# Columns of the weights' sums cast by ScalarE, spaced splits, and raw loads kept behind the conv tiles' loads

## The chip, the cores and the metric

The kernel runs on one core of a Trainium2 chip. The metric is the device time of one execution in microseconds. A core has five engines that run side by side, each in the order of its own instructions: TensorE (PE, matmuls, with its weight loads as PEld), VectorE (DVE), ScalarE (ACT), GpSimd (POOL) and SyncE (SP), which here issues the DMAs. They wait for each other through semaphores.

## The reference

One encoder block on x of 1024 tokens by 1024 channels in float32. Cut to what matters here:

```python
u = rms_norm(x, norm1_g)
q, k, v, cb, cc, ch, ga, gb = split(u @ w_in)
y_a = neighbourhood_attention(q, k, v, rpb) @ w_attn_branch
y_b = short_gated_conv(cb, cc, ch, conv_w) @ w_conv_branch
merged = sigmoid(ga) * y_a + sigmoid(gb) * y_b
x = x + merged @ w_o
h = rms_norm(x, norm2_g) @ w_mlp_in
x = x + square(relu(h)) @ w_mlp_out
```

The change touches the work on the gates `ga`, `gb` and on the two branch products.

## The kernel before, in words

float32 matmuls are done as float16 ones: each operand is split in a high half and a low half (`hi = fp16(w * s)`, `lo = fp16(w * s - hi)`), and products hi·hi, hi·lo and lo·hi are added in PSUM. A unit of 128 channels by 512 tokens is 12 matmuls of 128x512 in the gates and the attention branch, and 6 in the conv branch. The scale `s` of a weight chunk is a power of two made from the sum of the squares of the chunk. Parts of the products go by sums of blocks (a fast form with seven products, `seven`), so the splits are made of the raw weights, of their sums `gsum` (POOL, L1325) and, for the conv branch, of raw blocks added by POOL (L1414).

The preparation of a chunk goes like this. SP loads 128x1024 float32 weights into a `raw` buffer (L269, `load_now`; `due` decides when one is put in SP's program). ACT scales them by rows (L1201) where a norm belongs in, and takes squares with a sum for each partition (L1210, and L1396 for the conv branch). DVE adds the two or four sums of a partition (L1178, L394), and casts the result to one bf16 column of the tile `ones` (L1179, L396). PE multiplies a 128x128 block of ones by this column (L236 in `all_sum`), which adds over the partitions. DVE makes the scale from that (L239, then L495 to L502 or L160 to L163 and L327, and L1402 for the conv branch). Then come the splits: ACT casts the high half (L1343), DVE subtracts for the low half (L1339); `parts` gives them out in turn, a high half ahead of the low half before it. For the attention branch weights (`w_wa`) the two are L367 and L354, and their row sums of squares are one DVE reduction of 128x1024 (L386).

The stage is from about 310 to 560 us. Its PE program is written by loops: `gate_units(n)` makes the units of gate chunk n with the weights `w_s`; `a_unit` those of the attention branch with `w_wa`; `ab(j)` the units of both branches, in an order such as `"bb0b1bbb2b3"`, where b is a conv unit (weights `w_wb`, tile `bT`, which SP loads from the DRAM tile `bf`, L1519) and a digit an attention unit. The preparation steps are generators (`prep_s`, `prep_b`, `Chunk.prep`), put in a background queue `bg`; `tick` and `apart` place their instructions between the units by the number of PE columns that have been issued (6144 columns are a unit of 12 matmuls of 512). So the position of each instruction on its engine is fixed when the program is built, and an instruction that waits holds up all behind it on its engine. `cA[j]` are the attention branch chunks, `prep_b(j)` the conv branch's, and `prep_s(n)` the gates'. At the end of a chunk's use the sigmoid runs on ACT (L1498, tile `sg`, after sums on DVE at L1487 to L1496). Early in the stage, ACT and DVE also make the conv tiles: L943, L946, L961 to L988 on `bT`, `zb`, `mH`, `mL`.

Of the kernel before, what the change touches and what calls it, by code (L numbers as in the profile page):

```python
# [12 lines left out]
BF16 = mybir.dt.bfloat16  # L13
I32 = mybir.dt.int32
AF = mybir.ActivationFunctionType
# [86 lines left out]
def encoder_block(ctx: ExitStack, tc: tile.TileContext, x, weights, cols, gqk, rel, masks, out):  # L102
# [108 lines left out]
    def apart(mark, n=3, of=units):  # L211
        while of[0] < mark + n and not forced[0]:
            yield WAIT

    def built(*chs):
# [9 lines left out]
            tick()  # L225
            step()
        forced[0] = False
    ones, turn = base.tile([128, 132], BF16, name="ones"), [0]
    V.memset(ones, 1.0)

    def ones_col():
        turn[0] = (turn[0] + 1) % 4
        return ones[:, 128 + turn[0]:129 + turn[0]]

    def all_sum(a, out, bk, floor, lag=1):
        T.matmul(bk[:, 0:1], ones[:, 0:128], a, start=True, stop=True)  # L236
        yield
        yield from apart(units[0], lag)
        V.tensor_scalar(sc[:, out], bk[:, 0:1], floor, None, op0=OP.max)  # L239
        yield  # L240
# [27 lines left out]
        m = ch.widths[p][0] * ch.widths[p][1]  # L268
        SP.dma_start(t, bass.AP(tensor=weights.tensor, offset=weights.offset + ch.offs[p], ap=[[m, 128], [1, m]]))  # L269

    pend, deferring = [], [False]

    def due():
        while pend and (forced[0] or pend[0][0] <= work[0]):
            load_now(pend.pop(0)[1])

    def load_upto(n):
# [14 lines left out]
    class Chunk:  # L292
# [11 lines left out]
        def prep(self):  # L304
# [2 lines left out]
            rm, a, b, s = (cols_of("prep", i) for i in (nk, 1, 1, 1))  # L307
            self.inv = keep()
            tot = sum(k * w for k, w in self.widths)
            if self.kind in "QKCG":  # L310
                self.parts = wsp.tile([128, 2, tot], F16, name="w16_ws", tag="ws")
                for p, (k, w) in enumerate(self.widths):
                    while len(self.raw) <= p:
                        yield WAIT
                    A.activation(self.parts[:, 1, :k * w].bitcast(BF16), self.raw[p][:, :k * w], AF.Square,
                                 accum_out=sc[:, at(rm, p)])
                    yield
                V.tensor_reduce(sc[:, a], sc[:, at(rm, 0, n)], axis=AX, op=OP.add)
                c = ones_col()
                V.tensor_tensor(c, sc[:, a], sc[:, gm2], op=OP.mult)  # L320
                yield from apart(units[0], {"Q": 2, "C": 2, "K": 1}.get(self.kind, 3))
                yield from all_sum(c, b, bank(self.bank) if self.bank else anybank(), 1e-36)
                yield from pow2_half(b, 14, s, self.inv, more=self.more)
            else:
                yield from self.largest(rm, a, b)
                yield from pow2(b, 14, s, self.inv, False, more=self.more)
# [1002 lines left out]
        ch.sum = sum_of(sm)  # L1329
        yield  # L1330

    def parts(todo, s, then):

        scale = (lambda n: s[n]) if isinstance(s, list) else lambda n: s
        prev = None
        for n, it in enumerate(todo + [None]):
            if prev:
                o, w = prev
                V.scalar_tensor_tensor(o(1), w, sc[:, scale(n - 1)], o(0), op0=OP.mult, op1=OP.subtract)  # L1339
                then(n - 1)  # L1340
            if it:
                o, w = it
                A.activation(o(0), w, AF.Copy, scale=sc[:, scale(n)])  # L1343
            prev = it
            yield

    def forms_split(ch, t, s, P, turned=False):

        def then(n):
            if n == 1 and ch is not c1[0]:  # L1350
                done[0] += 2
                load_upto(done[0] + 5)
        r = ch.r
        todo = [(0, 1, r[0][:, 0:1]), (1, 3, r[1]), (3, 5, t[:, 0:2]), (5, 7, t[:, 2:4])]
        if turned:
            todo[2:] = todo[:1:-1]
        yield from parts([((lambda i, a=a, b=b: P[:, a:b, i]), w) for a, b, w in todo], s, then)

    gates = [0]

    def prep_s(n):

        ch = cS[n]
        if n == 1:
            while ch.s is None:
                yield WAIT
            s = ch.s
        else:
            yield from rows_scaled(ch, g1)
            sm = yield from squares(ch, M[0][:, 7].bitcast(BF16))  # L1370
            yield from apart(work[0], 2 * 6144, work)
            am = sum_of(sm)
            yield
            s, ch.inv = yield from scale_of(am, 9, 2)
        while done[0] < ch.first or n > 1 and not cS[n - 1].split or gates[0] < n - 1:
            yield WAIT
        t = w3p.tile([128, 4, 512], F32, name="gsum", bufs=1)
        yield from forms_sum(ch, t, None)
        if n > 1:
            yield from apart(work[0], 6144, work)  # L1380
        ch.P = wsp.tile([128, 7, 2, 512], F16, name="w16_s", tag="ws")
        yield from forms_split(ch, t, s, ch.P, n == 1)
        ch.split = True

    PB, pairs = {}, [0]
# [1 line left out]
    def prep_b(j):  # L1387

        ch = cB[j]
        while not ch.raw or not rowed[0] or not aged(ch, 0):  # L1390
            yield WAIT
        raw = ch.raw[0]
        w = raw.rearrange("p (a e n c) -> p e n a c", a=2, e=2, n=2)
        sm, rm = cols_of("prep", 2), cols_of("prep", 2)
        for a in range(2):
            A.activation(M[0][:, 7, :512].bitcast(BF16), raw[:, 512 * a:512 * a + 512], AF.Square,  # L1396
                         scale=sc[:, at(rowsB, a)], accum_out=sc[:, at(sm, a)])
        yield from apart(work[0], 2 * 6144, work)
        am = sum_of(sm)
        yield  # L1400
        s, ch.inv = yield from scale_of(am, 0, 3 if j else 2)
        V.tensor_scalar(sc[:, rm], sc[:, at(rowsB, 0, 2)], sc[:, s], None, op0=OP.mult)  # L1402
        yield
        while pairs[0] < j or done[0] < ch.first:
            yield WAIT
        P = PB[j] = wab.tile([128, 7, 2, 256], F16, name="w16_wb", tag="wb", bufs=1)

        def place(f, g, a):
            return lambda i: P[:, f:g, i, 128 * a:128 * a + 128]
        yield from parts([x for a in range(2) for x in ((place(0, 1, a), w[:, 0, 0:1, a]), (place(1, 3, a), w[:, 1, :, a]))],  # L1410
                         [at(rm, a) for a in (0, 0, 1, 1)], lambda n: None)
        for o, x_, y_ in (((0, 0), (0, 0), (0, 1)), ((0, 1), (0, 1), (1, 1)), ((1, 1), (0, 0), (1, 1)),
                          ((1, 0), (1, 1), (1, 0))):
            G.tensor_tensor(w[:, o[0], o[1]], w[:, x_[0], x_[1]], w[:, y_[0], y_[1]], op=OP.add)  # L1414
        yield from apart(work[0], 2 * 6144 if j else 6144, work)
        yield from parts([x for a in range(2) for x in ((place(3, 5, a), w[:, 0, :, a]), (place(5, 7, a), w[:, 1, :, a]))],
                         [at(rm, a) for a in (0, 0, 1, 1)], lambda n: None)
        done[0] += 1
        load_upto(done[0] + 5)
        ch.split = True  # L1420
# [150 lines left out]
    def ab(j):  # L1571
        n, P, ps = 2 * j, PB[j], {}
        z = [zb[:, i] for i in range(4)]

        def post2():
            V.tensor_tensor(z[0], ps[2], z[1], op=OP.add)
            times(n, 0)

        def post7():
            V.tensor_tensor(z[2], ps[7], z[1], op=OP.add)  # L1580
            V.tensor_tensor(z[1], ps[5], z[1], op=OP.subtract)
            V.tensor_tensor(z[3], ps[5], z[2], op=OP.subtract)
            V.tensor_tensor(z[2], ps[4], z[2], op=OP.add)
            times(n, 1)
            times(n + 1, 1)

        def post3():
            V.tensor_tensor(z[1], ps[3], z[1], op=OP.add)
            times(n + 1, 0)
        posts = {1: lambda: A.activation(z[1], ps[1], AF.Copy),  # L1590
                 6: lambda: V.tensor_tensor(z[1], ps[6], z[1], op=OP.add), 2: post2, 7: post7, 3: post3}

        def b_unit(o):
            i = ORDB[o]
            w = {5: 6, 6: 5}.get(SEVEN[i][1], SEVEN[i][1])
            act = SLOT[:, (7 * j + o) % 4]
            ps[i] = anybank()
            unit(group(ps[i], [(P[:, w, sw, 128 * a:128 * a + 128], act[:, a, sa]) for a in range(2)
                               for sw, sa in PASSES]), posts.get(i), 2, 4)
            land(7 * j + o + 4)  # L1600
        order = "bb0b1bbb2b3"
        if j == 0:
            order = "bb2b3bbbb"
        o = 0
        for c in order:
            if c == "b":
                b_unit(o)
                o += 1
            else:
                a_unit(n + int(c) // 2, int(c) % 2)  # L1610
        pairs[0] = j + 1

    tick(8)
    bg.append(prep_s(1))
    tick(2)
    fg.append(first_forms())
    bg.append(prep_b(0))
    for j in range(1, 4):
        bg.append(prep_s(2 * j))
        push(cA[j])  # L1620
# [690 lines left out]
```

## Time and profile before

| | us |
|---|---|
| three runs, median | 1216.38 |
| three runs, lowest and highest | 1215.01, 1217.11 |
| the profiled execution | 1214.99 |
| its span in the trace | 1213.2 |
| busy: PE | 1191.6 |
| busy: PEld | 574.6 |
| busy: DVE | 962.0 |
| busy: ACT | 777.8 |
| busy: POOL | 482.3 |

Busy times are sums over the span of one engine; PE is busy in 98% of it. Register, branch, semaphore and DMA-issuing instructions are not counted. The mean granted clock of PE was 0.994. Times in rows of the trace are from the span's start. In a row such as `ps_d<-ones`, the name at the left is the tile that is written, the ones at the right are read.

### The profile page before, as it was taken

The page shows a single profiled execution, that of the slowest core. Times are in us where ns is not written, and L with a number is a line of the kernel's source. Part 1 is how long each engine was busy: PE and PEld are TensorE (multiplying, and loading weights), DVE is VectorE, ACT ScalarE, POOL GpSimd, SP SyncE. Part 2 cuts the span into 40 slices and gives each one's busy share as a digit, 9 for nine tenths or more (in the row PEclk, how much of TensorE's full clock was granted, in tenths as well). Part 3 has the DMA queues.
Part 4 walks back from the last instruction along what each step waited for, and adds up shares of the span by engine and source line. Part 5 has one row for each costly group of instructions (what it writes and reads, how often), then busy time and mean ns, then how long its engine had stood idle before and what let it go on. Part 6 is the DMA issues. An engine that isn't in the chain of part 4 may idle for free.

```text
span 1213.2 us, 17139 instructions
## 1 busy us (share of the span) xinstructions
PE 1191.6 (98%) x6248; PEld 574.6 (47%) x6248; DVE 962.0 (79%) x1793; ACT 777.8 (64%) x1241; POOL 482.3 (40%) x314
## 2 busy tenths in 40 slices
PE   8999999999988998999999999999999999999998
PEld 7444444445433443444458444444444444444444
DVE  7987877898778887877878656456448989999998
ACT  7775668778656755436668787687775754646440
POOL 5610020221424360411003765665657562464472
PEclk9999999999998999999999999999999999999999
DMA  7755646787774424315096555355375924435212
GB/s 264 196 156 117 112 108 123 146 159 134 152 277 154 156 72 148 129 61 234 17 184 157 182 191 175 125 178 178 123 280 181 354 106 170 174 109 224 101 38 105
DMA packets 168373, 189.62 MB, mean 156 GB/s; under 512 B 123616, under 2 KB 124128, under 8 KB 164192
## 3 DMA queue, kind: packets, MB, share of 16 engines
q1 hardware_dynamic: 168288, 188.52, 52.0%
q8 instruction: 49, 0.80, 0.3%
q14 instruction: 36, 0.29, 0.1%
HBM read 117.19 MB, written 41.42 MB: 131 GB/s over the span
## 4 chain that ended last, share of the span: by engine, by line
PE 87%; DVE 8%; ACT 2%; issue 1%; POOL 1%; DMA 1%; DVEq 0%; ACTq 0%; POOLq 0%
PE ps_d L245 26%; PE ps_s L245 23%; PE ps_o L245 19%; PE ps_d L1166 9%; PE ps_d L695 2%; PE ps_d L744 2%; PE ps_s L744 2%; DVE w_s L1339 2%; PE ps_s L695 2%; PE ps_o L1147 1%; PE ps_s L1071 1%; POOL gsum L1325 1%; DVE w_wb L1339 1%; ACT raw L1201 1%; DMA bT<-bf 1%
## 5 line engine op out<-in xcount | busy, mean ns | idle before, releaser
L245 PEld LDWEIGHTS <-ops 128*128 128x128 f16 x1356 | 132.4, 98 | 157.3
L245 PEld LDWEIGHTS <-w 128*128 128x128 f16 x1368 | 132.8, 98 | 139.5
L1166 PE MATMUL ps_d<-uT,w_ws 128*128 128x512 f16 x576 | 127.9, 379 | 0.0
L245 PE MATMUL ps_s<-ops 128*128 128x512 f16 (+1 forms) x528 | 119.7, 377 | 0.0
L245 PE MATMUL ps_d<-ops 128*128 128x512 f16 x480 | 110.1, 379 | 0.0
L2132 ACT ACTIVATE ops<-hf,sc 128x2048 f16<-128x2048 f32 x26 | 52.0, 1998 | 84.8 <-PE ps_s L245 37.7
L1325 POOL TENSOR_TENSOR tsum<-raw 128x512 f32<-128x512 f32 x28 | 48.2, 1737 | 139.6 <-DVE v L1760 74.1
L1710 POOL TENSOR_TENSOR as<-as 128x512 f32<-128x512 f32 x60 | 82.9, 1381 | 41.6 <-ACT as L1992 38.1
L245 PEld LDWEIGHTS <-w_s 128*128 128x128 f16 x588 | 58.0, 100 | 80.8 <-issue 16.0
L1166 PEld LDWEIGHTS <-w_ws 128*128 128x128 f16 x576 | 54.5, 98 | 65.2 <-issue 1.0
L245 PE MATMUL ps_d<-u2T,w 128*128 128x512 f16 (+1 forms) x360 | 78.8, 368 | 0.0
L245 PE MATMUL ps_o<-ops 128*128 128x512 f16 (+1 forms) x348 | 78.6, 375 | 0.0
L2134 DVE SCALAR_TENSOR_TENSOR ops<-hf,sc,ops 128x2048 f16<-128x2048 f32 x26 | 74.4, 2861 | 3.3 <-ACT ops L2132 3.2
L245 PE MATMUL ps_o<-u2T,w 128*128 128x512 f16 (+1 forms) x348 | 76.0, 368 | 0.0
L245 PE MATMUL ps_s<-u2x,w 128*128 128x512 f16 (+1 forms) x336 | 74.5, 371 | 0.0
L1201 ACT ACTIVATE raw<-raw,sc 128x256 f32<-128x256 f32 x164 | 67.8, 493 | 1.9 <-DMA raw<-in_weights 1.9
L1343 ACT ACTIVATE w<-raw,sc 128x512 f16<-128x512 f32 (+1 forms) x28 | 24.6, 927 | 51.0 <-DVE sc L501 51.0
L2025 DVE TENSOR_TENSOR as<-ps_s,as 128x512 f32<-128x512 f32 x13 | 9.0, 692 | 57.9 <-ACT as L2044 57.9
L2148 POOL TENSOR_TENSOR raw<-raw 128x1024 f32<-128x1024 f32 x8 | 30.8, 3868 | 36.6 <-DVE ops L2142 36.6
L245 PEld LDWEIGHTS <-mH 128*128 128x128 f16 x304 | 29.6, 98 | 30.5
L2106 POOL TENSOR_TENSOR t<-raw,w2x 128x1024 f32<-128x1024 f32 x6 | 18.7, 3114 | 62.0 <-DMA w2x<-in_weights 62.0
L2138 ACT ACTIVATE ops<-raw,sc 128x1024 f16<-128x1024 f32 x24 | 26.3, 1138 | 26.6 <-DVE sc L152 19.2
(441 smaller groups left out, 2744.3 us busy)
## 6 DMA issues: line engine op xcount, KB each, us to landing
raw<-in_weights SPq DMA_DIRECT2D x89, 512.0 KB, 5.5
hs<-as SPq DMA_DIRECT2D x16, 1792.0 KB, 8.0
hf<-hs SPq DMA_DIRECT2D x26, 1024.0 KB, 6.2
bT<-bf SPq DMA_DIRECT2D x28, 512.0 KB, 4.5
w2x<-in_weights SPq DMA_DIRECT2D x16, 512.0 KB, 7.8
raw<-in_weights SPq DMA_DIRECT2D x16, 384.0 KB, 3.6
xt<-in_x SPq DMA_DIRECT2D x8, 512.0 KB, 10.9
gs<-s SPq DMA_DIRECT2D x4, 1024.0 KB, 4.4
```

The costliest lines, as they stand in the source:

```text
L245: T.matmul(ps, l, r, start=a, stop=b)
L695: T.matmul(ps, UT[:, sa, k, b * 128:(b + 1) * 128], w, start=(kind, k) == ("hh", 0), stop=(kind, k) == ("hl", 7))
L744: T.matmul(vbank["q", b], UT[:, sa, k, b * 128:(b + 1) * 128], cQ.parts[:, sw, 512 * k:512 * k + 512], start=(k, n) == (0, 0), stop=(k, n) ...
L1166: T.matmul(ps, l, r, start=a, stop=b)
L1201: A.activation(v, v, AF.Copy, scale=sc[:, at(g, 4 * i + k)])
L1325: G.tensor_tensor(t[:, o], a, b, op=OP.add)
L1339: V.scalar_tensor_tensor(o(1), w, sc[:, scale(n - 1)], o(0), op0=OP.mult, op1=OP.subtract)
L1710: sub.tensor_tensor(z[o], z[a], z[b], op=op)
L2132: A.activation(P[:, 1, 0], hf, AF.Copy, scale=sc[:, Rs])
L2134: V.scalar_tensor_tensor(P[:, 1, 1], hf, sc[:, Rs], P[:, 1, 0], op0=OP.mult, op1=OP.subtract)
L2138: A.activation(P[:, 0, 0, 1024 * i2:1024 * i2 + 1024], w[i2], AF.Copy, scale=sc[:, fw])
L2148: G.tensor_tensor(w11[i2], w11[i2], w12[i2], op=OP.add)
```

## The change

1. The column of a weights' sum is no longer added and cast on DVE. `summed(sums)` casts the two or four partial sums on ACT into two or four columns of `ones`, and `all_sum` multiplies each column on PE and adds them in PSUM. `prep_s` (from chunk 2), `prep_b` and `cA[1]` to `cA[3]` use it. For these `cA` the sums of squares are four ACT squares of 128x256 in place of the DVE reduction.
2. The waits in columns between the squares and the sum go away; in their place the sum is put at once behind the cast, and the `ones` matmul where the distance from it says.
3. Splits of `prep_s` (from chunk 2) and `prep_b` are spaced (`gap=1`): the high halves of a pair or a group on ACT, then 6144 columns of PE work, then the low halves on DVE.
4. In `ab`, raw loads are kept out of SP's program while the first conv tiles' loads are put in (`behind`).
5. `prep_b(0)` is put in the queue ahead of `prep_s(1)`, with two more ticks.

In counts: ACT gets 25 more instructions of the kind ACTIVATE (13 casts, 12 squares), DVE loses 16 reductions and 13 casts, PE gets 19 more `ones` matmuls with their weight loads; POOL and SP have as many instructions as before.

```diff
-    ones, turn = base.tile([128, 132], BF16, name="ones"), [0]
+    ones, turn = base.tile([128, 148], BF16, name="ones"), [0, 0]
...
+    def summed(sums):
+        n = sums.stop - sums.start
+        if turn[1] + n > 16:
+            turn[1] = 0
+        turn[1] += n
+        a = 132 + turn[1] - n
+        nc.scalar.activation(ones[:, a:a + n], sc[:, sums], AF.Copy)
+        return [ones[:, a + i:a + i + 1] for i in range(n)]
+
     def all_sum(a, out, bk, floor, lag=1):
-        T.matmul(bk[:, 0:1], ones[:, 0:128], a, start=True, stop=True)
+        a = a if isinstance(a, list) else [a]
+        for i, c in enumerate(a):
+            T.matmul(bk[:, 0:1], ones[:, 0:128], c, start=i == 0, stop=i == len(a) - 1)
...
     def due():
-        while pend and (forced[0] or pend[0][0] <= work[0]):
+        while pend and not (behind[0] and not forced[0]) and (forced[0] or pend[0][0] <= work[0]):
             load_now(pend.pop(0)[1])
...
-            if self.kind in "QKCG":
+            if self.kind == "A" and self is not cA[0]:
+                while not self.raw or not aged(self, 0):
+                    yield WAIT
+                sm = cols_of("prep", 4)
+                for i in range(4):
+                    A.activation(M[0][:, 7, :256].bitcast(BF16), self.raw[0][:, 256 * i:256 * i + 256], AF.Square,
+                                 scale=sc[:, at(self.rows, i)], accum_out=sc[:, at(sm, i)])
+                c = summed(sm)
+                yield
+                yield from apart(work[0], 3 * 6144, work)
+                yield from all_sum(c, b, anybank(), 1e-36)
+                yield from pow2_half(b, 14, s, self.inv)
+            elif self.kind in "QKCG":
...
-    def parts(todo, s, then):
+    def parts(todo, s, then, gap=0):
 
+        if gap:
+            get = (lambda n: s[n]) if isinstance(s, list) else lambda n: s
+            for n, (o, w) in enumerate(todo):
+                A.activation(o(0), w, AF.Copy, scale=sc[:, get(n)])
+                yield
+            yield from apart(work[0], gap * 6144, work)
+            for n, (o, w) in enumerate(todo):
+                V.scalar_tensor_tensor(o(1), w, sc[:, get(n)], o(0), op0=OP.mult, op1=OP.subtract)
+                then(n)
+                yield
+            return
...
-            sm = yield from squares(ch, M[0][:, 7].bitcast(BF16))
-            yield from apart(work[0], 2 * 6144, work)
-            am = sum_of(sm)
-            yield
-            s, ch.inv = yield from scale_of(am, 9, 2)
+            sm = cols_of("prep", 2)
+            for i in range(2):
+                A.activation(M[0][:, 7].bitcast(BF16), ch.raw[i], AF.Square, accum_out=sc[:, at(sm, i)])
+                yield
+            c = summed(sm)
+            s, ch.inv = yield from scale_of((c, work[0]), 9, 3)
...
-        yield from apart(work[0], 2 * 6144, work)
-        am = sum_of(sm)
-        yield
-        s, ch.inv = yield from scale_of(am, 0, 3 if j else 2)
+        c = summed(sm)
+        yield
+        s, ch.inv = yield from scale_of((c, work[0]), 0, 3 if j else 2)
...
             land(7 * j + o + 4)
+            behind[0] = o < 2
+        behind[0] = True
         order = "bb0b1bbb2b3"
...
     tick(8)
-    bg.append(prep_s(1))
+    bg.append(prep_b(0))
+    tick(2)
+    bg.insert(0, prep_s(1))
     tick(2)
     fg.append(first_forms())
-    bg.append(prep_b(0))
```

Two places show how instructions move. The first is ACT about 326 to 342 us, from the row scales of a raw gate chunk on (`raw<-raw`). The casts `w_wb` are the high halves of the first conv branch weights, `L1210` and, after, `L1411` the squares of gate chunk 2. Line numbers after are 11 to 40 higher. Before:

```order
L1201 ACTIVATE raw<-raw,sc 128x2x128 x4
L943 ACTIVATE mH<-bT 128x512 x2
L1481 ACTIVATE sg<-raw 128x512
L1478 ACTIVATE sg<-ps_d,sc 128x512
L943 ACTIVATE mL<-bT 128x512 x4
L1201 ACTIVATE raw<-raw,sc 128x2x128 x4
L1210 ACTIVATE mH,sc<-raw 128x1024 x2
L1201 ACTIVATE raw<-raw,sc 128x2x128 x4
L1509 ACTIVATE sg<-ps_s 128x512
L1343 ACTIVATE w_wb<-raw,sc 128x128
```

And after, from the squares of `cA[1]` on, which stand right behind the first of those row scales:

```order
L326 ACTIVATE mH,sc<-raw,sc 128x256 x4
L241 ACTIVATE ones<-sc 128x4
L966 ACTIVATE mH<-bT 128x512 x2
L1518 ACTIVATE sg<-raw 128x512
L1515 ACTIVATE sg<-ps_s,sc 128x512
L966 ACTIVATE mL<-bT 128x512 x4
L1360 ACTIVATE w_wb<-raw,sc 128x128
L1360 ACTIVATE w_wb<-raw,sc 128x2x128
L1360 ACTIVATE w_wb<-raw,sc 128x128
L1360 ACTIVATE w_wb<-raw,sc 128x2x128
L1224 ACTIVATE raw<-raw,sc 128x2x128 x4
L1411 ACTIVATE mH,sc<-raw 128x1024 x2
```

The four `w_wb` casts were behind the squares of gate chunk 2 and are now ahead of them and of the row scales before these; the cast `L241 ACTIVATE ones<-sc 128x2` for the sum follows right behind the last row. `cA[1]`'s squares and its cast of four columns are new in the row.

The second place is SP from about 342 to 373 us, in `ab(0)`: the loads of conv tiles (`bT`) and of raw weights. Before:

```order
L1519 DMA bT<-bf 128x2048 x4
L269 DMA raw<-in_weights 128x1024
L1519 DMA bT<-bf 128x2048 x2
L269 DMA raw<-in_weights 128x1024 x2
L1519 DMA bT<-bf 128x2048
L269 DMA raw<-in_weights 128x1024
L1519 DMA bT<-bf 128x2048 x4
```

After:

```order
L1556 DMA bT<-bf 128x2048 x4
L280 DMA raw<-in_weights 128x1024
L1556 DMA bT<-bf 128x2048 x3
L280 DMA raw<-in_weights 128x1024 x3
L1556 DMA bT<-bf 128x2048 x4
```

The seventh `bT` load stood behind two raw loads and has moved ahead of them; the three raw loads now go out together.

More of the change, by code (lines that the diff above doesn't have):

```diff
@@ L269, in load_into @@
         SP.dma_start(t, bass.AP(tensor=weights.tensor, offset=weights.offset + ch.offs[p], ap=[[m, 128], [1, m]]))
-    pend, deferring = [], [False]
+    pend, deferring, behind = [], [False], [False]
     def due():
-        while pend and (forced[0] or pend[0][0] <= work[0]):
+        while pend and not (behind[0] and not forced[0]) and (forced[0] or pend[0][0] <= work[0]):
             load_now(pend.pop(0)[1])
@@ L1345, in parts, with forms_split @@
             yield
-    def forms_split(ch, t, s, P, turned=False):
+    def forms_split(ch, t, s, P, turned=False, spaced=False):
         def then(n):
@@ L1356, in forms_split @@
             todo[2:] = todo[:1:-1]
+        if spaced:
+            at_p = [((lambda i, a=a, b=b: P[:, a:b, i]), w) for a, b, w in todo]
+            yield from parts(at_p[:2], s, lambda n: then(n), 1)
+            yield from parts(at_p[2:], s, lambda n: None, 1)
+            return
         yield from parts([((lambda i, a=a, b=b: P[:, a:b, i]), w) for a, b, w in todo], s, then)
@@ L1378, in prep_s @@
         yield from forms_sum(ch, t, None)
-        if n > 1:
-            yield from apart(work[0], 6144, work)
         ch.P = wsp.tile([128, 7, 2, 512], F16, name="w16_s", tag="ws")
-        yield from forms_split(ch, t, s, ch.P, n == 1)
+        yield from forms_split(ch, t, s, ch.P, n == 1, n > 1)
         ch.split = True
@@ L1410, in prep_b @@
         yield from parts([x for a in range(2) for x in ((place(0, 1, a), w[:, 0, 0:1, a]), (place(1, 3, a), w[:, 1, :, a]))],
-                         [at(rm, a) for a in (0, 0, 1, 1)], lambda n: None)
+                         [at(rm, a) for a in (0, 0, 1, 1)], lambda n: None, 1)
         for o, x_, y_ in (((0, 0), (0, 0), (0, 1)), ((0, 1), (0, 1), (1, 1)), ((1, 1), (0, 0), (1, 1)),
@@ L1416, in prep_b @@
         yield from parts([x for a in range(2) for x in ((place(3, 5, a), w[:, 0, :, a]), (place(5, 7, a), w[:, 1, :, a]))],
-                         [at(rm, a) for a in (0, 0, 1, 1)], lambda n: None)
+                         [at(rm, a) for a in (0, 0, 1, 1)], lambda n: None, 1)
         done[0] += 1
```

## The prediction

> **What bounds the kernel now.** I began with the table of busy time by stretch, then the waits of TensorE (PE), and then followed each wait to the engine that ended it. The first view shows, for each stretch, the span and PE's busy time, then PEld, VectorE (DVE), ScalarE (ACT) and GpSimd (POOL), the granted clock, the DMA share and GB/s.
>
> ```profile
> 309.00:345.00 36.00, 30.80 (x143) 13.81 (x142) 30.88 (x49) 28.22 (x53) 14.70 (x12) 0.98 0.79 225
> 345.00:400.00 55.00, 49.96 (x218) 21.87 (x217) 46.27 (x101) 35.00 (x62) 24.89 (x22) 0.92 0.45 157
> 400.00:460.00 60.00, 56.42 (x266) 25.50 (x264) 48.47 (x100) 33.63 (x59) 24.88 (x18) 1.00 0.38 123
> ```
>
> PE lacks 5.20, 5.04 and 3.58 us there, 13.82 us in all. So PE sets the time, and in this stage it is stopped by others. All that the change can win is here. The waits of PE from 300 to 670 us name the four places:
>
> ```profile
> PE ps_d L245 <- DMA bT<-bf: 5.0, 1, 5.0
> PE ps_o L236 <- DVE ones L1179: 3.6, 1, 3.6
> PE ps_d L236 <- DVE ones L396: 3.6, 1, 3.6
> PE ps_d L236 <- DVE ones L1179: 1.6, 1, 1.6
> ```
>
> Three are the one-column `ones` matmul of a weights' sum (L236) behind DVE's cast; one is a conv tile `bT`. Past 460 us the list has nothing. PE's timeline has start, length, and in brackets the idle time before a row:
>
> ```profile
> 327.35 0.16 PE L236 MATMUL ps_d<-ones 128*128 128x1 bf16 x1 [1.55 <-DVE ones L1179]
> 327.38 2.75 PE L245 MATMUL ps_s<-uT,w_s 128*128 128x512 f16 x12
> 335.14 0.17 PE L236 MATMUL ps_o<-ones 128*128 128x1 bf16 x1
> ...
> 344.16 0.16 PE L236 MATMUL ps_o<-ones 128*128 128x1 bf16 x1 [3.65 <-DVE ones L1179]
> 344.26 4.04 PE L245 MATMUL ps_d<-uT,w_s 128*128 128x512 f16 x12
> ...
> 350.74 1.46 PE L245 MATMUL ps_d<-bT,w_wb 128*128 128x512 f16 x6
> ...
> 362.39 1.46 PE L245 MATMUL ps_s<-bT,w_wb 128*128 128x512 f16 x6
> 368.89 2.74 PE L245 MATMUL ps_d<-bT,w_wb 128*128 128x512 f16 x6 [5.04 <-DMA bT<-bf]
> 371.42 3.93 PE L245 MATMUL ps_s<-uT,w_s 128*128 128x512 f16 x11
> 375.40 0.17 PE L236 MATMUL ps_o<-ones 128*128 128x1 bf16 x1
> 385.82 0.16 PE L236 MATMUL ps_d<-ones 128*128 128x1 bf16 x1
> ...
> 419.53 1.46 PE L245 MATMUL ps_s<-bT,w_wb 128*128 128x512 f16 x6
> ...
> 458.32 0.16 PE L236 MATMUL ps_d<-ones 128*128 128x1 bf16 x1 [3.58 <-DVE ones L396]
> 458.34 4.12 PE L245 MATMUL ps_s<-uT,w_s 128*128 128x512 f16 x12
> ...
> 479.50 1.46 PE L245 MATMUL ps_s<-bT,w_wb 128*128 128x512 f16 x6
> ```
>
> A full unit of 12 matmuls is 2.75 us long (pitch 2.59), one of 6 is 1.46 (pitch 1.29). After the 1.55 us pause nothing slows. After 3.65 the unit takes 4.04 (+1.29); after 5.04 one of 6 takes 2.74 (+1.28) and the next goes from 371.42 to 375.40, 3.98 for 2.59 (+1.39); after 3.58 one takes 4.12 (+1.37). So the four places cost 13.82 + 5.33 = 19.15 us.
>
> Who is late is seen on the other engines. DVE at the second place, and the DMA queue of SP at the third:
>
> ```profile
> 339.99 0.23 DVE L1402 TENSOR_SCALAR sc<-sc 128x2 f32<-128x2 f32 x1
> 342.28 1.57 DVE L1339 SCALAR_TENSOR_TENSOR w_wb<-raw,sc,w_wb 128x128 f16<-128x128 f32 x4 [2.07 <-ACT w_wb L1343]
> 343.95 0.16 DVE L1179 CAST ones<-sc 128x1 bf16<-128x1 f32 x1
> ```
>
> ```profile
> 352.23 1.61 SPq L1519 DMA_DIRECT2D bT<-bf  x2
> 360.56 1.91 SPq L269 DMA_DIRECT2D raw<-in_weights  x2
> 362.56 0.38 SPq L1519 DMA_DIRECT2D bT<-bf  x1
> ```
>
> DVE had idled for ACT's `w_wb` casts with the little `ones` cast queued behind their splits. On SP, two raw loads stood ahead of a `bT` load and went out only at 360.56 to 362.47, when the `w_s` splits had let their buffers go.
>
> **The change, part by part.** All places are in times of before. ACT's rows carry the sum (the last fence is its 128x2 form from the groups by shape: busy, mean ns):
>
> ```profile
> 320.00 0.70 ACT L1396 ACTIVATE mH<-raw,sc 128x512 bf16<-128x512 f32 x1
> ...
> 325.81 1.69 ACT L1201 ACTIVATE raw<-raw,sc 128x256 f32<-128x256 f32 x4
> 335.97 1.69 ACT L1201 ACTIVATE raw<-raw,sc 128x256 f32<-128x256 f32 x4
> 339.69 0.19 ACT L1210 ACTIVATION_READ_ACCUMULATOR mH<-raw 128x1 f32 x1
> 356.61 2.00 ACT L1498 ACTIVATE sg<-sg,sc 128x2048 f32<-128x2048 f32 x1 [8.36 <-DVE sg L1496]
> 368.05 0.19 ACT L1210 ACTIVATION_READ_ACCUMULATOR mH<-raw 128x1 f32 x1
> 392.49 1.49 ACT L1343 ACTIVATE w_wb<-raw,sc 128x128 f16<-128x128 f32 x4 [5.11 <-DVE sc L1402]
> 414.44 1.99 ACT L1498 ACTIVATE sg<-sg,sc 128x2048 f32<-128x2048 f32 x1
> 420.54 0.19 ACT L1210 ACTIVATION_READ_ACCUMULATOR mH<-raw 128x1 f32 x1
> 477.12 0.19 ACT L1210 ACTIVATION_READ_ACCUMULATOR mH<-raw 128x1 f32 x1
> ```
>
> ```profile
> L482 ACT ACTIVATE sc<-sc 128x2 f32<-128x2 f32 x3 | 0.6, 203 | 2.2 <-DVE sc L481 2.2
> ```
>
> *Unit prices.* An ACT cast of 128x2 or 128x4 is 0.20 us by that row; 13 of them are 2.6 us in an engine that idles 8.36 us before one row, so only their place counts. A square of 128x256 with its sum lies between a 128x256 scale with a 0.19 read (1.69 / 4 + 0.19 = 0.61) and the 128x512 square (0.70 + 0.19 = 0.89); I take 0.65, since four share a line with the first, so 2.6 for four. A `ones` matmul more is the step from 385.82 to the next unit, 0.03 us: 19 more are 0.6. DVE loses 29 small or middling operations; its cover is not needed where it is no longer waited for, so I give that nothing of its own.
>
> *First place, 327.35.* The sum of `prep_b(0)` now comes one gate unit after 310 us, when ACT has its two squares and the cast behind it: 1.55 gone. But `cA[1]`'s sum now has its four `ones` columns after the first `w_s` unit. PE is there at 327.38 + 2.59 − 1.55 = 328.4; ACT has the four scales from 325.81 (to 327.4), four squares (2.6) and a cast (0.2): 330.2. New stall 1.8 (0, if the four squares hide in a wait, to 2.8), too short to slow the clock.
>
> *Second place, 344.16.* `prep_s(2)`'s sum now needs its columns one unit earlier. PE comes there at 335.14 + 0.25 (1.8 for 1.55) + 0.1 + 2.59 = 338.1. ACT starts at 335.97 the four `w_wb` casts (1.49), which now stand ahead of the scales and squares, then the work from 335.97 to 339.88 (3.91) and the cast: 341.6. The `w_wb` casts wait for L1402's scale on DVE; its sum leaves PE 20 us earlier than now, but it stands behind DVE's conv work, which I put 0.4 after 335.97: 342.0. Stall 3.9, and a slow unit of 1.3 as after 3.65. Three units are left instead of two: 342.0 + 1.3 + 3 × 2.59 = 351.1, where the conv unit of 350.74 was. So up to here 0.3 lost. Ends: nothing, if DVE clears 4 us sooner; and, with the scale at its present 339.99, 340.2 + 1.49 + 3.91 + 0.2 = 345.8, that is 7.7 + 1.3 = 9.0. What decides is the queue of ACT, whose casts for the conv weights wait; I lie nearer to 335.97 since the sum is early.
>
> [...] The trace: 3.58, 3.65 and 5.04 all slowed, 1.55 did not; so I charge it.
>
> *Third place, 368.89.* The raw loads now go out after `bT`. The `bT` load then waits only for the unit that reads its buffer, which ends at 357.3; the pair at 352.23 took 3.9 us to land, the late one 6.3 beside raw loads: 361.2 to 363.7, needed at 362.39 + 1.29 = 363.7. So 5.04 and 2.67 go. SP's three raw loads move past one `bT`; they are issued when the splits release them, about as now, and feed sums much later. Next is `prep_s(3)`'s `ones`, which follows the last conv unit: PE at 363.7 + 1.29 + 0.3 = 365.3. ACT's squares end at 368.24 now, less 1.75 since the two first `w_s` casts move into the 8.36 us before 356.61, plus 0.2: 366.7. Stall 1.4 (0 to 3.1).
>
> *Fourth place, 458.32.* `cA`'s sum leaves DVE (L386 and the chain behind the sigmoid sum) and is done on ACT before PE gets there: 3.58 and 1.37 go.
>
> *Other places that move.* `prep_s(5)`'s `ones` comes four units earlier, after 419.53, while ACT's squares end at 420.73 now; with the sigmoid (414.44) ahead of the `w_wa` casts, about 421.5 with the cast. Stall 2.0 (0 to 3.5 with 1.3 behind it). `prep_s(7)`'s comes after 479.50 + 1.29 = 480.8; ACT ends its squares at 477.31, now behind a sigmoid of 2.0 and a copy of 0.5: 480.0 at best, 483.2 if the sigmoid waits for its sum; the middle of 0 to 2.4 is about 1.0. The spaced splits delay the low halves by one unit (2.59), which nothing waits for where PE is several units off.
>
> *Sum.* Gone 19.15; new 1.8 + 3.9 + 1.3 + 1.4 + 2.0 + 1.0 + 0.6 = 12.0. Gain 7.15. The profiled execution took 1214.99 (span 1213.2), which gives 1207.8; it is the lower end of the three runs, whose median is 1216.38, so I predict 1209.2.
>
> **The rivals.** *No new stalls.* ACT has its columns before PE at every moved place; DVE is freed of 1.2 us reductions and the splits no longer alternate with ACT, which speaks for it; against it stands ACT's order at 335.97. Then 1216.4 − 19.15 + 0.6 = 1197.9; with the stalls halved 1203.5.
>
> *ACT takes DVE's place and eats the gain.* If each moved sum is late by its upper end at two of the three places with clock cost (9.0 at the second, 4.8 for `prep_s(5)`), with 1.8, 1.4, 1.0 and 0.6: 18.6, so 1215.8: no change.
>
> *Slower.* The scale L1402 for `w_wb` stays as late as now, and the squares behind those casts in ACT's queue with it: 9.0 at the second place, and at 392.49, where ACT waits 5.11 for it, `cA[2]`'s four squares follow: 392.49 + 1.49 + a reduction of 1.2 + 2.6 + 0.2 = 398.0, when PE, ahead by 6.3 us after the third place, would come by 392.2: 5.8 and 1.3. With 1.8, 1.4, 2.0, 1.0 and 0.6 that is 22.9, 3.8 over what is won: 1220.1. It decides when the new stalls pass 19.15 + 2.4. Against it: both sums now leave PE earlier.
>
> *The edit does not do its work on `bT`.* If the load still lands at 368.84, the third place stays (7.7) but `prep_s(3)`'s stall goes: 1209.2 + 7.7 − 1.4 = 1215.5. Nothing but the reader of its buffer is ahead of it, so this is unlikely.
>
> **How the numbers follow.** Within 0.2% (1213.9 to 1218.8), which a measurement of this kernel can hardly tell from none, counts as the same. My sum has 0.52 (1204 to 1213.9), few new stalls 0.24 (1197 to 1204), the eaten gain 0.11 and the unmoved `bT` 0.03 (same), slower 0.10. So faster 0.76, same 0.14, slower 0.10. From 1199.5 to 1216.5 about 0.16 is left out: 0.12 above and 0.04 below.
>
> **What would show it.** Right: no wait of PE on a DVE `ones`, none on `bT` at 364; waits on ACT `ones` instead, some 2 us after the first `w_s` unit and near 4 three units later, with one slow unit; PE busy in 345 to 400 up by 5 or more; the conv units again beginning near 351; smaller waits by ACT near 365, 413 and 472. Wrong: the L1402 scale on DVE, or a `gsum` split, as PE's releaser; a `bT` wait that is back at another unit; or the conv units beginning at 345 or at 355, which would be the first or the third rival.

## The result: 1216.2 to 1210.4 us, and the profile after

The changed kernel took 1210.41 us (median of four runs, 1209.48 to 1211.59), beside 1216.18 for the kernel before: a ratio of 0.9954, 95% interval 0.9936 to 0.9971, 5.8 us less. The forecast was 1209.2, the range 1199.5 to 1216.5. The profiled execution was the longest of the four, 1211.59 with a span of 1209.8.

PE's waits over 0.3 us in the changed kernel from 300 to 670 us (total, times, longest):

```profile
PE ps_s L247 <- ACT ones L241: 7.3, 2, 3.7
PE ps_d L247 <- ACT ones L241: 1.8, 1, 1.8
```

All four waits of before are gone, and three new ones stand on ACT's cast. The windows (span, then busy time of PE, PEld, DVE, ACT, POOL, granted clock, DMA share, GB/s) show PE's loss at 345 to 400 us gone, from 5.04 to none, and the others about as large as they were (5.60 and 3.60):

```profile
309.00:345.00 36.00, 30.40 (x143) 13.48 (x142) 28.52 (x44) 30.82 (x66) 19.08 (x16) 0.95 0.72 219
345.00:400.00 55.00, 55.00 (x258) 24.67 (x257) 43.53 (x95) 40.06 (x77) 24.52 (x19) 0.97 0.46 163
400.00:460.00 60.00, 56.40 (x261) 25.17 (x260) 45.74 (x103) 41.15 (x78) 19.44 (x16) 0.94 0.38 124
```

PE's timeline after, at the places that the prediction named:

```profile
326.25 2.75 PE L256 MATMUL ps_s<-uT,w_s 128*128 128x512 f16 x12
330.84 0.24 PE L247 MATMUL ps_d<-ones 128*128 128x1 bf16 x4 [1.83 <-ACT ones L241]
...
342.61 0.19 PE L247 MATMUL ps_s<-ones 128*128 128x1 bf16 x2 [3.74 <-ACT ones L241]
342.82 5.28 PE L256 MATMUL ps_o<-qD,w_s 128*128 128x512 f16 x12
347.90 3.02 PE L256 MATMUL ps_d<-uT,w_s 128*128 128x512 f16 x12
350.75 2.75 PE L256 MATMUL ps_s<-s4T,w_s 128*128 128x512 f16 x12
353.34 1.46 PE L256 MATMUL ps_d<-bT,w_wb 128*128 128x512 f16 x6
...
367.59 0.19 PE L247 MATMUL ps_s<-ones 128*128 128x1 bf16 x2
...
393.64 0.24 PE L247 MATMUL ps_d<-ones 128*128 128x1 bf16 x4
...
418.22 0.19 PE L247 MATMUL ps_s<-ones 128*128 128x1 bf16 x2 [3.60 <-ACT ones L241]
418.27 2.72 PE L256 MATMUL ps_o<-bT,w_wb 128*128 128x512 f16 x6
420.79 2.77 PE L256 MATMUL ps_d<-bT,w_wb 128*128 128x512 f16 x6
423.35 2.84 PE L256 MATMUL ps_s<-qD,w_wa 128*128 128x512 f16 x12
...
476.78 0.19 PE L247 MATMUL ps_s<-ones 128*128 128x1 bf16 x2
```

New are 1.83 us at 330.84; 3.74 at 342.61 with two slow units behind it (342.82 to 350.75 is 7.93 for 2 × 2.59, 2.75 too long; the granted clock was 0.50 from 342.61 to 347.90 and 0.91 from there to 350.75); and 3.60 at 418.22 with two slow conv units (418.27 to 423.35 is 5.08 for 2 × 1.29, 2.50 too long; the granted clock was 0.50 there). That is 14.4 us where 19.15 were; 19 more `ones` matmuls take 0.3 to 0.6 by an estimate from the steps to the next unit, 0.05 us behind two columns (418.22 to 418.27), 0.10 behind four (330.84 to 330.94) and 0.02 to 0.03 behind the one of before (458.32 to 458.34, 327.35 to 327.38). So the trace pair should differ by about 4.3 us in this stage, and does: from the start of the first `w_wa` unit to the start of the last `w_s` unit 222.5 us became 218.3. Over the whole span the pair differs by only 3.4 us (1213.2 to 1209.8), mainly since PE reached this stage 0.6 us later. The medians lie further apart, 5.8 us, because the profiled execution of before was 1.2 us under its median and that of the changed kernel 1.2 over: in the four runs of the changed kernel the mean granted clock was 0.997 twice (1209.48 and 1209.64 us) and 0.994 twice (1211.18 and 1211.59, the one profiled), so some 2 us come and go between runs of one program.

### The profile page after: what moved, and what is told of

Read it like the earlier page. It is cut to its first block, busy times and chain, and to the rows that moved or that the text cites. A ratio compares the mean times of both kernels' runs of the same rounds, so it can differ in the third digit from the quotient of the medians.

```text
span 1209.8 us, 17188 instructions
## 1 busy us (share of the span) xinstructions
PE 1192.8 (99%) x6267; PEld 575.7 (48%) x6267; DVE 947.9 (78%) x1767; ACT 785.8 (65%) x1278; POOL 480.9 (40%) x314
## 4 chain that ended last, share of the span: by engine, by line
PE 61%; DVE 4%; ACT 2%; DMA 2%; issue 1%; POOL 0%; SPq 0%; DVEq 0%
PE ps_d L256 23%; PE ps_s L256 21%; PE ps_o L256 16%; DMA raw<-in_weights 1%; DVE w_s L1364 1%; DMA x<-in_x 1%; DVE mL L1504 0%; DVE sc L409 0%; ACT raw L1224 0%; ACT mH L326 0%; ACT sg L1535 0%; DVE sc L1701 0%; ACT mH L1411 0%; ACT mL L1493 0%; DVE w_wb L1364 0%
## 5 line engine op out<-in xcount | busy, mean ns | idle before, releaser
L256 PE MATMUL ps_d<-u2x,w 128*128 128x512 f16 (+1 forms) x204 | 43.0, 360 | 0.0
```

The lines of the kernel that those rows point to most:

```text
L256: T.matmul(ps, l, r, start=a, stop=b)
```

## Experiments

Each was compared with runs of the kernel before on the same chip (medians 1216.42, 1215.98 and 1216.67 in the three groups). The line numbers of a variant lie within a few of the changed kernel's, or of those before.

**1. The second place's sum one unit later.** In `prep_s` of the changed kernel:

```diff
-            s, ch.inv = yield from scale_of((c, work[0]), 9, 3)
+            s, ch.inv = yield from scale_of((c, work[0]), 9, {2: 4}.get(n, 3))
```

> The changed kernel, with the ones columns of gate chunk 2 asked for one unit later (four units instead of three behind the cast). Theory, the places are independent and each costs its pause plus its slow units: the 3.74 us pause at 342.6 shrinks by the 2.59 us unit to about 1.15, too short to slow the clock (1.55 and 1.83 did not), so 2.59 and the 2.75 us of slow units go: 1210.4 - 5.3 = 1205.1 us. Rival, ScalarE and VectorE bound the stage and the pauses are only where it shows: PE then waits as much more at the next places (367, 375 or 386 us, or 4 to 6 us more at 418) and the time stays near 1210.

Measured 1210.26 us (ratio to before 0.9949, 0.9937 to 0.9962). Locally as the first theory had it, and nothing for the whole. PE's waits in it, beside the unchanged 1.83:

```profile
PE ps_s L247 <- ACT ones L241: 6.7, 2, 5.0
PE ps_o L247 <- ACT ones L241: 1.2, 1, 1.2
```

The pause fell to 1.15 without a slow unit, so conv began at 348.56, 4.8 us earlier. Then 1.66 at the next sum (364.64), and 5.03 instead of 3.60 at gate chunk 5's, gave most of it back; PE came to the third conv phase only 1.1 us earlier.

**2. Gate chunk 5's sum two units later**, the same edit with `{5: 5}`.

> The changed kernel, with the ones columns of gate chunk 5 asked for two units later, as late as before the change (four conv or attention units on). Theory of independent places: the pause of 3.60 us at 418 and the 2.58 us of slow units behind it go, 1210.4 - 6.2 = 1204.2 us. Rival, bound by ScalarE: a pause of 3 us or more comes back at that sum or at the three sums near 443 us, and the time stays near 1210.

Measured 1208.52 us (0.9939, 0.9927 to 0.9952). The wait at 418 us and its slow units went (6.1 us), and one of 2.87 with 1.7 of slow units came at gate chunk 7's sum (the row also holds the 3.74 at the second place):

```profile
PE ps_s L247 <- ACT ones L241: 6.6, 2, 3.7
```

Of the 6.1 us some 1.9 stayed as gain. The rival had named another sum.

**3. The loads alone.** The kernel before with `behind` in `due` and `ab`, nothing else:

```diff
-        while pend and (forced[0] or pend[0][0] <= work[0]):
+        while pend and not (behind[0] and not forced[0]) and (forced[0] or pend[0][0] <= work[0]):
...
             land(7 * j + o + 4)
+            behind[0] = o < 2
+        behind[0] = True
```

> The kernel before, with only the raw loads kept behind the first conv loads. Theory of independent places: the wait on bT and its slow units go (5.04 + 2.67 us), the three waits on VectorE's ones stay at 1.6, 3.6 and 3.6: 1216.2 - 7.7 = 1208.5 us. Rival, what PE wins there is given back at the next sum on VectorE (the cast L396 at 458 us, whose pause would grow from 3.6 to 8 or more): near 1215.

Measured 1216.0 us (0.9997, 0.9989 to 1.0006): nothing. The wait on `bT` did go; these are the queue of SP and PE's timeline of this kernel:

```profile
352.60 5.50 SPq L1519 DMA_DIRECT2D bT<-bf  x3
360.87 8.24 SPq L269 DMA_DIRECT2D raw<-in_weights  x3
```

```profile
364.06 1.46 PE L245 MATMUL ps_d<-bT,w_wb 128*128 128x512 f16 x6
...
370.98 0.16 PE L236 MATMUL ps_o<-ones 128*128 128x1 bf16 x1 [2.87 <-DVE ones L1179]
372.91 5.28 PE L245 MATMUL ps_d<-qD,w_s 128*128 128x512 f16 x12 [1.77 <-DVE zb L1582]
```

PE went through the conv units without a stop and stood two units later: 2.87 and 1.77, and 2.48 of slow clock, 7.1 of the 7.7 us that were won. The rival was right, but for the place.

**4. The changed kernel without the loads' part.**

> The changed kernel without keeping the raw loads behind the conv loads. Theory of independent places: the wait on bT is back at 5 us with slow units, and all else stays: 1210.4 + 7.7 = 1218.1 us. Rival, the pause at gate chunk 5's sum (3.60 and 2.58 slow) was there only because PE had come earlier by the bT wait: it goes when bT waits, 1210.4 + 7.7 - 6.2 = 1211.9 us.

Measured 1210.79 us (0.9952, 0.9939 to 0.9966), as with it, and neither theory had it: no wait on `bT` came back. SP's queue in it:

```profile
355.03 1.61 SPq L1556 DMA_DIRECT2D bT<-bf  x2
356.75 0.85 SPq L280 DMA_DIRECT2D raw<-in_weights  x2
360.21 0.33 SPq L1556 DMA_DIRECT2D bT<-bf  x1
```

The same two raw loads stand ahead of the seventh `bT`, as before the change, but went out at 356.75 and not at 360.56. The first `w_s` halves of gate chunk 2 are made earlier, and so their buffers came free before the `bT` load was due: ACT casts the first high half at 350.95, ahead of the sigmoid (354.47), where before it was at 359.00 and behind it (356.61). The spacing is not what does this, for with the splits in turn (experiment 7) the first one stands at 350.74 too; it goes with the earlier sum.

**5. Four sums later.** 1 and 2 together, with chunk 7's sum two units and `cA[1]`'s one unit later:

```diff
-            s, ch.inv = yield from scale_of((c, work[0]), 9, 3)
+            s, ch.inv = yield from scale_of((c, work[0]), 9, {2: 4, 5: 5, 7: 5}.get(n, 3))
...
-                yield from apart(work[0], 3 * 6144, work)
+                yield from apart(work[0], (4 if self is cA[1] else 3) * 6144, work)
```

> The changed kernel, with the ones columns of cA[1] and gate chunk 2 asked for one unit later and those of gate chunks 5 and 7 two units later. Independent places: the pauses at 331, 342 and 418 us with their slow units go (1.83, 5.3 and 6.2 us) and 473 us stays free, 1197 us. Chain theory (the pauses show how far ScalarE and VectorE are behind, and what PE wins is lost at the next sum, as the first two runs showed): PE pauses at 365 to 395 us or at the sums near 440 us instead, and only what the single moves gave adds up, 0 to 2 us: 1207 to 1209 us.

Measured 1202.74 us (0.9890, 0.9874 to 0.9906): the best kernel here, 13 us under before, and more than the single moves had given. PE's waits over 0.3 us in it:

```profile
PE ps_o L247 <- ACT ones L241: 3.2, 1, 3.2
PE ps_s L247 <- ACT ones L241: 2.0, 1, 2.0
```

Two are left, at 342.40 and 364.59 us, and none over 0.3 us past 365. In this kernel, with most sums placed where their cast is ready, little of what is won at one place is lost at another. The chain theory of this run forecast too little, the other too much. Two of the four moves, those of `cA[1]` and of chunk 7, were not run alone, so their share is not known.

**6. The sums on VectorE again**, in the places of the changed kernel: `summed` adds and casts on DVE.

```diff
-        nc.scalar.activation(ones[:, a:a + n], sc[:, sums], AF.Copy)
-        return [ones[:, a + i:a + i + 1] for i in range(n)]
+        b, c = cols_of("prep", 1), ones_col()
+        V.tensor_reduce(sc[:, b], sc[:, sums], axis=AX, op=OP.add)
+        V.tensor_copy(c, sc[:, b])
+        return [c]
```

> The changed kernel, but the partial sums are added and cast by VectorE into one column (as before the change), everything else and every place of a ones matmul as in the changed kernel. If the cast's move off VectorE's queue is what wins: each pause at a sum grows by VectorE's queue, 1 to 4 us at three or more places, and the gain of 5.8 us is gone: 1214 to 1217 us. If the new places of the sums, the spacing or the loads win, it stays at 1210 to 1211 us.

Measured 1219.19 us (1.0026, 1.0017 to 1.0036): slower than before. DVE's timeline shows why:

```profile
331.09 0.16 DVE L237 TENSOR_REDUCE sc<-sc 128x1 f32<-128x4 f32 x1 [1.49 <-ACT mH L323]
...
344.69 0.15 DVE L237 TENSOR_REDUCE sc<-sc 128x1 f32<-128x2 f32 x1 [3.52 <-ACT mH L1408]
344.88 0.16 DVE L238 CAST ones<-sc 128x1 bf16<-128x1 f32 x1
344.95 1.40 DVE L1361 SCALAR_TENSOR_TENSOR w_wb<-raw,sc,w_wb 128x128 f16<-128x128 f32 x4
...
426.54 0.16 DVE L237 TENSOR_REDUCE sc<-sc 128x1 f32<-128x2 f32 x1 [3.81 <-ACT mH L1408]
```

The pauses of PE at these two sums are 5.65 and 5.74 us. The queue is the other way round from what I expected: not the sum waits for DVE's work, but DVE stands still for 3.5 and 3.8 us at the little reduction until ACT has its squares, and the `w_wb` splits wait behind it. The sums at these two stops follow ACT's squares by 0.4 us, hardly later than with the cast on ACT (0.3). What makes the pause at 345 us longer is mostly the stop of 1.49 us before it, at `cA[1]`'s sum: DVE's conv work and the `w_wb` scale come later behind it (339.10, where the changed kernel has 336.76), and with them ACT's `w_wb` casts (339.36 for 337.01) and the squares behind these. The longer stops delay what follows them, such as the `w_wb` splits from 338.75 to 344.95. On ACT the cast stands behind the squares that it reads, on the same engine, and holds up nobody: in the changed kernel it takes 0.20 us at 342.35, and ACT goes on without idle time at 342.46.

**7. Splits in turn again**: the changed kernel with `spaced` false and `gap` 0 everywhere.

> The changed kernel with the splits in turn (high, low, high, low) instead of spaced by a unit. If the spacing carries the gain, since ScalarE no longer waits for VectorE between high halves: 1214 to 1216 us, with the pauses at 342 and 418 us longer. If not, 1209 to 1211 us, with the same pauses.

Measured 1225.76 us (1.0081, 1.0067 to 1.0096), 15 us over the changed kernel, far more than expected. PE's longest waits in it, and the first `w_s` casts:

```profile
PE ps_s L247 <- ACT ones L241: 6.4, 3, 3.7
PE ps_o L247 <- ACT ones L241: 4.6, 1, 4.6
PE ps_s L256 <- DVE sg L1582: 3.5, 1, 3.5
```

```profile
350.74 1.76 ACT L1377 ACTIVATE w_s<-raw,sc 128x512 f16<-128x512 f32 x2 [4.76 <-DVE sc L524]
```

The pauses at 331 and 342 us were the same (1.83 and 3.74); new ones came at a sum at 367 us, and on DVE's work for the conv and attention units (3.50 and 1.94). Since the sums after 350 us also got other places by this edit, it does not tell the spacing's own price. Nor does it put back a wait of one unit ahead of the gate splits, which the change also takes out (see experiment 10).

**8. `cA`'s sums of squares on VectorE again.**

```diff
-            if self.kind == "A" and self is not cA[0]:
+            if False:
```

> The changed kernel, but the attention branch chunks' sums of squares are again one VectorE reduction of 128x1024 with a cast there. If that reduction in VectorE's queue costs what the trace of before showed at 458 us: the pause of 1.83 us at 331 us goes and one of 3 to 5 us comes at gate 2's sum (390 us) or at 440 us: 1212 to 1215 us. If the reduction is hidden: 1208.5 to 1210.5 us.

Measured 1212.32 us (0.9969, 0.9958 to 0.9981), 1.9 over the changed kernel. The pause at `cA[1]`'s sum is 4.25 us on DVE's cast (with 1.7 of slow units) instead of 1.83; not at 390 or 440 us, and the one at chunk 5's sum 6.25 us. At `cA[1]` the reduction ends at 329.9, and DVE does four conv operations before its cast at 332.76.

**9. The cast alone.** The kernel before with `sum_of` casting on ACT into columns; the places of the sums as before.

> The kernel before, with only the partial sums of gate and conv chunks cast by ScalarE into columns (the ones matmuls stay where they are, cA stays on VectorE, splits in turn, loads as before). If the cast's move off VectorE's queue wins by itself: the pauses of 1.55 and 3.65 us with 1.3 of slow units at 327 and 344 us go, 1216.2 - 6.5 = 1209.7 us. If what PE wins there is lost at the next wait (bT at 364 us, L396 at 458 us): 1214 to 1216.5 us.

Measured 1214.81 us (0.9986, 0.9977 to 0.9995), 1.9 less. The pause at 327 us fell to 0.26. At 344 us PE still waited 4.00. The profile names a transfer (`bf<-mL`), but ACT's squares had ended at 340.39 and its cast at 343.93, just ahead of PE's step at 343.99: placed where it was, it stood behind four row scales, a copy into `sg` and four `w_wb` casts in ACT's queue as it had stood behind splits in DVE's. The wait on `bT` stayed at 3.92. The one at 458 us was gone, but one of 2.38 with 1.7 of slow units came at a sum at 425.61.

**10. The spacing alone**, on the kernel before (sums on DVE). The edit brings one thing more, as the change does: `prep_s` no longer waits one unit before its splits.

```diff
-        if n > 1:
-            yield from apart(work[0], 6144, work)
```

> The kernel before, with only the splits of weights spaced by a unit. If the spacing wins by itself, since high halves no longer wait for VectorE and the raw buffers come free sooner: the bT wait (5.04 and 2.6) goes, and 1209 to 1212 us. If spacing only fits together with sums cast by ScalarE: VectorE's casts stay queued behind the splits, and 1215 to 1220 us.

Measured 1212.62 us (0.9969, 0.9958 to 0.9980), 4.0 less. PE's longest waits, and SP's queue:

```profile
PE ps_d L236 <- DVE ones L1179: 5.0, 2, 3.5
PE ps_o L245 <- DVE w_s L1341: 3.1, 1, 3.1
PE ps_d L245 <- DVE sg L1501: 2.0, 1, 2.0
PE ps_d L245 <- DVE w_wb L1341: 1.3, 1, 1.3
```

```profile
352.55 3.46 SPq L1533 DMA_DIRECT2D bT<-bf  x3
362.73 4.72 SPq L269 DMA_DIRECT2D raw<-in_weights  x3
```

The waits at 344 us, on `bT` and on L396 are gone. In their place PE waits for low halves (`w_s`, `w_wb` by L1341), which now come later, and 3.46 at a sum at 375.33. So the spacing, together with the wait taken out, gives the larger part of the gain by itself. The `bT` wait went as my first theory had it, but not for its reason: the raw loads go out later than before (362.73), not sooner, and the seventh `bT` load, the last of the three in the row, now stands ahead of them.

**11. Two more sums later.** The kernel of experiment 5 with `{2: 5, 3: 4, 5: 5, 7: 5}`.

> As the kernel with four sums later (1202.7 us), with the sum of gate chunk 2 one more unit later (five) and that of chunk 3 one unit later (four). Its pauses left were 3.15 us at 342 and 1.99 with 1.69 of slow units at 365. Independent places: 2.6 and 3.7 us go, 1196.5 us. Chain: the splits of gate 2 or gate 3 come later by as much, and PE waits for w_s or at a sum between 365 and 400 us: 1201 to 1206 us.

Measured 1210.82 us (0.9952, 0.9939 to 0.9964): all that experiment 5 had won over the changed kernel is lost. PE's longest waits in it:

```profile
PE ps_d L256 <- DVE zb L1619: 5.9, 1, 5.9
PE ps_s L256 <- ACT sg L1546: 1.9, 1, 1.9
```

The pause at 342 us fell to 0.55. But the later scale moved gate chunk 2's `w_s` splits behind the sigmoid on ACT, and on DVE 4.2 us of splits came to stand between the sums of the conv units; PE then waited 5.85 us for a bank that DVE had not read. Chain, but worse than I had put it.

**12. Experiment 5 without the loads' part.**

> As the kernel with four sums later (1202.7 us), without keeping the raw loads behind the conv loads. If the spacing already frees the raw buffers in time, as the run of the changed kernel without the loads' part showed (no wait on bT): 1202 to 1204 us. If the kernel, now that PE is 8 us earlier in this stage, does need it: the bT wait is back and 1206 to 1210 us.

Measured 1210.28 us (0.9946, 0.9932 to 0.9959). The time is that of the second expectation, the cause is not: no wait on `bT`, but one of 3.5 us at a sum at 419.87 us with 2.5 of slow units, and 1.8 on DVE. Loads put in SP's program at other times also shift the preparations that look for them (`aged`), so these sums stand at other units. The loads' part is worth about 7 us in this kernel (6.9 by the distances to the kernel before on each chip) and 0.4, less than can be told from nothing, in those of experiments 3 and 4.

## Why the prediction was right, and where it was not

**Likeliest case and sign.** Right: the time lies 1.2 us over the forecast, and the waits are where the text said, on ACT's `ones`. That it came so near is partly luck: stalls of 2.4 us that the sum had did not come, some 5.5 us that it lacked did, and the trace pair differs by 4.3 us in this stage where 7.15 was forecast. The conv units began at 353.34, between the 351 of the likeliest case and the 355 named as a sign against it. And the account of one term, the third place, missed a part of what moved there.

**First place.** 1.55 gone, and 1.8 forecast for `cA[1]`: measured 1.83, with no slow unit behind it (330.94 to 336.12 is 5.18 for 2 × 2.59). That a stall in its range is too short to slow the clock was my estimate from the 1.55 of before, and it does not hold up to the 2.8 where the range ended: in experiment 5 a pause of 1.99 us cost 1.7. The squares of 128x256 were 0.62 each (forecast 0.65), the casts 0.20.

**Second place.** 3.9 forecast, 3.74 measured, by the rows that the working used, with L1439's scale as the one thing that ACT waited for:

```profile
337.01 1.49 ACT L1360 ACTIVATE w_wb<-raw,sc 128x128 f16<-128x128 f32 x4 [2.02 <-DVE sc L1439]
338.41 1.69 ACT L1224 ACTIVATE raw<-raw,sc 128x256 f32<-128x256 f32 x4
...
342.35 0.20 ACT L241 ACTIVATE ones<-sc 128x2 bf16<-128x2 f32 x1
```

That scale's sum left PE 11.5 us earlier (315.85 for 327.35), not 20 as the working said, which was early enough. Mis-sized was the slow clock behind the pause: 1.3 forecast, as 3.65 had cost it before (granted clock 0.67 from 344.16 to 348.31), 2.75 measured. The mean granted clock differed between runs of the changed kernel (0.994 in two, 0.997 in two), and the length of a pause does not settle its cost: in experiment 2 a pause of 2.87 us was followed by 1.7 of slow units, and in experiment 5 one of 1.99 by 1.7. Here a pause of 2 us could cost slow units.

**Third place.** The wait on `bT` went as forecast, 7.7 us. But the step "the raw loads now go out after `bT`" was not needed for it: by itself that order takes the wait away (experiment 3, where the time was lost again further on), and without it the wait stays away too (experiment 4). What the working missed is "issued when the splits release them, about as now": in experiment 4 the first `w_s` cast comes 8 us sooner and its low half 5.4 us (354.35 for 359.74), and the raw loads go out 3.8 us sooner. This goes with the earlier sum and not with the spacing (experiment 7). The wait of one unit that was taken out is not enough for it either, for in experiment 10 the first `w_s` cast is still at 358.24, behind the sigmoid. Whether it is needed beside the earlier sum was not tried. The stall of 1.4 forecast for `prep_s(3)` didn't come: the cast was done at 364.47, PE came at 367.59.

**Fourth place.** Gone, as forecast: the four columns at 393.64 had no wait. It had cost 0.36 us more than the working counted, since before the change the unit behind the slow one, at 462.26, was slow too (3.11 for 2.75).

**Other places.** `prep_s(5)`: 2.0 forecast, 3.60 with 2.50 of slow units measured; this is the term that was sized worst. ACT's part, 8.1 us from the sigmoid's start to the cast, was as worked out (410.04 to 418.16):

```profile
410.04 2.00 ACT L1535 ACTIVATE sg<-sg,sc 128x2048 f32<-128x2048 f32 x1 [7.56 <-DVE sg L1533]
...
417.96 0.20 ACT L241 ACTIVATE ones<-sc 128x2 bf16<-128x2 f32 x1
```

```profile
396.14 0.69 DVE L1542 TENSOR_TENSOR sg<-ps_s,sg 128x512 f32<-128x512 f32 x1 [3.64 <-ACT sg L1546]
...
406.49 2.47 DVE L1364 SCALAR_TENSOR_TENSOR w_s<-gsum,sc,w_s 128x1024 f16<-128x1024 f32 x2
...
409.32 0.68 DVE L1533 TENSOR_TENSOR sg<-ps_o,sg 128x512 f32<-128x512 f32 x1
```

But ACT had idled 7.56 us for a sum on DVE. This one stood behind two low halves of `w_s`, as it had before the change, in a queue in which DVE had itself stood 3.64 us for ACT at 396.14. I had taken the sigmoid's start relative to PE from the trace of before. PE came to this place 5.1 us earlier than there (the conv unit ahead of the sum ends at 414.46, where it had ended at 419.53), but the sum on DVE only 3.4 us (409.32 for 412.70). `prep_s(7)`: 1.0 forecast, none measured.

**The sum.** Gone 19.15, as forecast; new 12.0 forecast, 14.4 and the small matmuls measured. What I had missed in the main shows in experiments 1, 3 and 11: I added the places up as if each cost its pause alone. While PE pauses the engines behind it catch up, and the next place is sized by what is left of that: in experiment 1, 2.6 us less at the second place, and no slow unit there, left 1.66 more at the next sum and 1.4 more at chunk 5's.

**What carried the gain.** Alone, the cast gives 1.9 us, the spacing with the wait taken out 4.0, and the loads 0.4. Taken out of the changed kernel, the cast loses 8.8, `cA`'s squares 1.9, the spacing up to 15.3 (the sums move with it) and the loads 0.4. So the parts do not add up, and need each other: with the early sums, both the cast on DVE (experiment 6) and the splits in turn (experiment 7) make the kernel slower than before. Left open is what `prep_b(0)` ahead of `prep_s(1)` does, and what the wait of one unit does; neither was tried by itself.

## What to carry to other kernels

In this kernel a small operation that joins two engines belonged on the engine that makes its operand: put early on another one, it stopped that engine's whole queue (experiment 6: 1.5, 3.5 and 3.8 us). Where several waits stand one behind the other, size the next wait with the time won before it taken off, and try all the moves together: two of them alone gave 0.2 and 1.9 us, four together 8. And look at the best version once more: later is not always better (experiment 11 gave the 8 us back).

## What was not expected of the hardware

In these traces the price of a pause on PE's clock has no fixed relation to its length. Single pauses up to 1.83 us cost at most 0.2 us in any of them (granted clock 1.00 from 330.84 to 333.50 in the changed kernel, behind 1.83). One of 1.89 (experiment 11) cost 1.6 us, one of 1.99 (experiment 5) 1.7, one of 2.02 (experiment 10) nothing; at one sum 3.15 (experiment 5) slowed no unit and 3.18 (experiment 12) cost 1.7; 3.74 at one place cost 2.8 in three kernels and 1.4 in the kernel of experiment 7; 5.03 to 6.25 cost 1.3 to 2.7. So for this kernel an estimate should carry 0 to 2.8 us for each pause of 1.9 us or more.
